# A hybrid decoder step in one program: keys kept transposed for the delta rule, the order of its streams, the memory output stage and the ffn norm

## The chip, the cores and the metric

The kernel runs on one core of a Trainium2 chip. The metric is device time in microseconds for one execution; lower is better. The median of three runs stands for a kernel.

## What is computed

One layer of a decoder for 512 prompt tokens and 32 sample tokens (544 columns), width 1024, in float32. Cut to what matters here:

```python
u = rmsnorm(h); qa, ka, va, qkv_b, z, beta, a, gate_a, gate_b = split(u @ w_in)
A = dilated window attention(qa, ka, va)
q, k, v = silu(causal_dwconv(qkv_b)); q, k = l2norm(q), l2norm(k)
B = gated_delta_chunked(q, k, v, beta, g, s0)      # 8 heads, 128 x 128 state
h += merge(A, B, gates) @ w_out
h += memory_attend(rmsnorm(h)) @ w_mem_o
h += conv_ffn(rmsnorm(h)); y = rmsnorm(h)
```

In the delta rule each head needs, per 128 tokens, a triangular system `M` (built from keys and decay), the values, the keys scaled by decay with tokens on the partitions (`k_dec`), and then a recurrence over four chunks that carries the state `St`.

## The kernel before, in words

All activations lie transposed, 128 features on the partitions and 544 tokens along the row. The weights come as blocks, most of them 128x1024, in the order of `plan()`. Each block is loaded (`wr`), split on ScalarE into a rounded high part `wh` and on VectorE into the rest `wl = wr - wh`, and `dense` (line 567) multiplies it: for each of 8 row groups k, three products (wh·xh, wh·xl, wl·xh) on two halves of 272 columns, so 48 matmuls a block into one of two wide PSUM tiles `pd`. The two split parts have two buffers each (`NHL = 2`), so block n+2 is split once block n has been multiplied.

Everything else is written as generators, the streams: dilated attention, the convolution of a delta head (`conv`, line 1038), the delta rule and the memory attention. After each row group `dense` calls `tick` (line 646). It lets streams take steps, smallest priority number first, while an account of the engines that the builder keeps (`_Account`, line 276) says that the step's inputs are there, that enough SBUF slots of the 53 are free, and that VectorE and ScalarE are no further behind TensorE than `LAG[prio]` us. Where slots run out, `reserve` and `drain` force steps. The order of every engine's instructions is thus fixed when the program is built; the engines then run it in order and wait for semaphores.

The delta rule of a group of four heads: `conv` makes `y`, the convolved q, k or v of a head; it is parked in HBM (`park`, line 501), and for q and k transposed on TensorE and squared for the norm. When q and k of four heads are there, `gdn_group` (line 1088) fetches them (`qk<-park`), builds M and the inner attention, and parks these. It then starts `gdn_solve` (a 32x32 triangular solve on VectorE), two `gdn_preps` and the finals. `gdn_prep` (line 1224) fetches Mt, kT and vT of a head (`ft<-park`), transposes each on TensorE (4 transposes of 128x128 into one PSUM bank), scales the transposed keys on ScalarE into `Kd` and the values into `Vr`, and makes the inverse `U`. `gdn_chain` (line 1321) is the recurrence: `xc` on VectorE from `St`, a product with U, `vn` on ScalarE, products with Kd and At, the new `St` on VectorE. `gdn_sample` does the sample tokens; its wide multiplies `sz` run on GpSimd.

`mem_out` (line 2191) is the output projection of the memory attention, blocks `mo` 0 to 3, two output tiles each: after each of the 8 products, `h += pd` on VectorE (the rows `xr<-xr,pd`, which free the wide tile), and `hstat` makes the split norm input `nh`, `nl` and adds squares to `hacc`. `ffn` (line 2205) starts with block `fg` 0, computes the norm in its midst with `rstd` (sums of squares per token by five products with a column of ones, square root on ScalarE, reciprocal on VectorE) and then `spread`s it over the partitions by five products with the identity; the result `rf` scales every product that follows (`fcb<-pd,rf`).

Of the kernel before, what the change touches and what calls it, by code (L numbers as in the profile page):

```python
# [17 lines left out]
D = 1024  # L18
# [384 lines left out]
class Builder:  # L403
    def __init__(self, nc, tc, I, O, ctx):
        self.nc, self.tc, self.I, self.O = _Engines(nc), tc, I, O
        self.acc = self.nc.acc
        self.clk = self.acc.at
        self.ring = {"b": [], "d": []}
        ec = ctx.enter_context
        self.cp = ec(tc.tile_pool(name="cp", bufs=1))  # L410
        self.wp = ec(tc.tile_pool(name="wp", bufs=1))
        self.sp = ec(tc.tile_pool(name="sp", bufs=1))
        self.tp = ec(tc.tile_pool(name="tp", bufs=1))
        self.pd = ec(tc.tile_pool(name="pd", bufs=2, space=PSUM))
# [4 lines left out]
        self.raw, self.hl = {}, {}  # L419
        self.next_load = self.next_split = 0  # L420
        self.streams, self.stores = [], []
        self.count = {"S": 0, "L": 0}
        self.cur = "b"
        self.nm = 0
        self.flags = {}
        n = 0
        self.src = []
        for b in self.plan:
            if b[0] == "fd":
                self.src.append(I[f"wd{b[1][0]}"][b[1][1]])  # L430
            else:
                self.src.append(I["w"][n]); n += 1
# [94 lines left out]
    def split_to(self, j):  # L527
        while self.next_split <= min(j, len(self.plan) - 1):
            n = self.next_split
            self.load_to(n + NAHEAD)  # L530
# [14 lines left out]
            self.nc.vector.tensor_tensor(lo, r, hi.bitcast(F32), OP.subtract)  # L545
            self.hl[n] = (hi, lo)
            self.hl.pop(n - NHL - 2, None)
            self.next_split += 1

# [11 lines left out]
    def weights(self, b, ahead=True):  # L561
        n = self.idx[b]
        self.split_to(n + (NHL - 1 if ahead else 0))
        return self.hl[n]
# [81 lines left out]
    def tick(self):  # L646
# [3 lines left out]
        self.flush()  # L650
        while c["PE"] - t0 < PE_SHARE:
# [47 lines left out]
    def rstd(self, accs, n):  # L699

        nc = self.nc
        c = (n + 127) // 128
        pb = self.bank((128, c))
        for t in range(c):
            o = min(128 * t, n - 128)
            nc.tensor.matmul(pb[:, t:t + 1], accs[0][:, o:o + 128], self.cst("ones")[:, 0:1], start=True, stop=True)
        return self.rroot(pb)

# [329 lines left out]
    def conv(self, kind, h, cb):  # L1038
# [20 lines left out]
        if kind < 2:  # L1059
            if g not in self.ssT:  # L1060
                self.ssT[g] = self.small(34, tag="w34", bufs=16)
            yield 0, 0
# [4 lines left out]
            for i in range(4):  # L1067
                c = 16 * (1 - kind) + 4 * i + hh
                nc.scalar.activation(self.small(128, tag="junk", bufs=2), pb[:, 128 * i:128 * i + 128], AF.Square, accum_out=self.ssT[g][:, c:c + 1])
        self.flag((kind, h))  # L1070

    def gdn_setup(self):
# [6 lines left out]
        self.ob, self.ssT, self.silz, self.gc = {}, {}, {}, {}  # L1079
# [8 lines left out]
    def gdn_group(self, g):  # L1088
# [89 lines left out]
        self.add(self.gdn_solve(g), 1, (2, 1), (2, 1), "gdn_group")  # L1178
        for e in range(NPREP):
            self.add(self.gdn_preps(g, range(e, 4, NPREP), Mt, At), 1, (3, 0), (6, 0), "gdn_group")  # L1180
# [3 lines left out]
    def gdn_preps(self, g, hs, Mt, At):  # L1184
        pre = None
        for hh in hs:
            if pre is None:
                pre = [self.fetch(d) for d in (Mt[hh], self.sil[1, 4 * g + hh], self.sil[2, 4 * g + hh])]
# [35 lines left out]
    def gdn_prep(self, g, hh, nx, Mts, At, pre):  # L1224
# [7 lines left out]
        Mt, kT, vT = pre[:3]  # L1232
        U = pre[3] if len(pre) > 3 else None
        del pre
        yield from self.on(Mt, kT, vT)
# [7 lines left out]
        yield 1, 0, 3, 0  # L1243
        Kd = self.s((128, 512), name="Kd")
        pb = self.bank()
        for sl in sls:
            nc.tensor.transpose(pb[:, sl], kT[:, sl], ident)
        for i in range(4):
            act(Kd[:, sls[i]], pb[:, sls[i]], AF.Copy, scale=c["kd"][:, cc[i]])
        yield 0, 0, 2, 0  # L1250
        pb = self.bank()
        for sl in sls:
            nc.tensor.transpose(pb[:, sl], vT[:, sl], ident)
        Vr = vT
# [3 lines left out]
        del vT  # L1258
# [55 lines left out]
        if nx is not None:  # L1314
            pre = [self.fetch(d) for d in (Mts[nx], self.sil[1, 4 * g + nx], self.sil[2, 4 * g + nx])] + [self.load_u(g, nx)]
        self.add(self.gdn_chain(g, hh, U, Kd, Vr, At.pop(hh), self.sil[0, h], kT), 1, (2, 0), (2, 0), "gdn_preps")
# [874 lines left out]
    def mem_out(self):  # L2191
        xs = list(zip(self.oh, self.ol))
        self.hstat_begin()
        ps = [self.wide() for _ in range(2)]
# [4 lines left out]
        for m in range(8):  # L2199
            o = ps[m][:, 256:800] if m < 2 else self.dv(self.dense(("mo", m // 2), xs, k0=4 * (m % 2), last=m % 2 == 1))  # L2200
            self.nc.vector.tensor_tensor(self.h[m], self.h[m], o, OP.add)
            self.hstat(m, "g_ffn", self.nc.gpsimd if m < 7 else None)


    def ffn(self):
# [121 lines left out]
    def main(self):  # L2327
# [9 lines left out]
        for n, (kind, k) in enumerate(MIX):  # L2337
# [3 lines left out]
            if kind in "gd" and tag not in seen:  # L2341
# [56 lines left out]
MAIN, PE_SHARE, LAG = 5, 2.5, {0: 4.5, 1: 2.5, 2: 2.5, 3: 1.5}  # L2398
# [52 lines left out]
```

## Time and profile before

| | |
|---|---|
| runs | 1245.27 us median of 3 (1244.31 to 1246.10) |
| profiled execution | 1244.79 us, its span 1243.0 us |
| TensorE busy | 1209.9 us, 97% of the span |
| VectorE, ScalarE, GpSimd busy | 714.5, 527.8, 163.0 us |
| DMA queue of the program | 232.95 MB, 54.4% of 16 engines |
| chain that ended last | TensorE 64%, VectorE 5%, DMA 4%, ScalarE 3%, issue 2% |

A matmul record lasts from its start to a modelled end, and records overlap, so the mean of a record is longer than the distance between two starts. Nearly every instruction has line 339, the recording layer's call; groups are told apart by the tiles they write and read.

### The profile page before, as it was taken

The page shows a single profiled execution, that of the slowest core. Times are in us where ns is not written, and L with a number is a line of the kernel's source. Part 1 is how long each engine was busy: PE and PEld are TensorE (multiplying, and loading weights), DVE is VectorE, ACT ScalarE, POOL GpSimd, SP SyncE. Part 2 cuts the span into 40 slices and gives each one's busy share as a digit, 9 for nine tenths or more (in the row PEclk, how much of TensorE's full clock was granted, in tenths as well). Part 3 has the DMA queues.
Part 4 walks back from the last instruction along what each step waited for, and adds up shares of the span by engine and source line. Part 5 has one row for each costly group of instructions (what it writes and reads, how often), then busy time and mean ns, then how long its engine had stood idle before and what let it go on. Part 6 is the DMA issues. An engine that isn't in the chain of part 4 may idle for free.

```text
span 1243.0 us, 26005 instructions
## 1 busy us (share of the span) xinstructions
PE 1209.9 (97%) x10498; PEld 1164.1 (94%) x10498; DVE 714.5 (57%) x1360; ACT 527.8 (42%) x1128; POOL 163.0 (13%) x352
## 2 busy tenths in 40 slices
PE   7999999999999999999999999999999999999997
PEld 7899998999999988988899998899999999999997
DVE  6635356766688845584675555565552455424564
ACT  5334434555544634665742344453331233313342
POOL 0000100311251220020000000022220022101210
PEclk9999999999999999999999999999999999999998
DMA  6332773446686569746394488364655555555322
GB/s 225 107 118 78 281 264 106 162 145 221 213 262 219 192 196 319 256 146 198 120 326 136 175 311 279 116 218 156 226 182 176 203 187 186 188 193 186 121 84 72
DMA packets 90693, 234.61 MB, mean 189 GB/s; under 512 B 25929, under 2 KB 31542, under 8 KB 89797
## 3 DMA queue, kind: packets, MB, share of 16 engines
q1 hardware_dynamic: 90574, 232.95, 54.4%
q8 instruction: 83, 1.36, 0.4%
q14 instruction: 36, 0.29, 0.1%
HBM read 199.47 MB, written 77.58 MB: 223 GB/s over the span
## 4 chain that ended last, share of the span: by engine, by line
PE 64%; DVE 5%; DMA 4%; ACT 3%; issue 2%; SPq 1%; POOL 0%; POOLq 0%; DVEq 0%; ACTq 0%
PE pd L339 52%; PE b L339 12%; DVE wl L339 1%; DMA z<-park 1%; SPq L339 1%; DMA ft<-park 1%; ACT wh L339 1%; DMA qk<-park 1%; DVE y L339 1%; DMA mkv<-mkT 0%; DVE xr L339 0%; DMA wr<-in_w 0%; DVE st L339 0%; DMA usol<-su 0%; DVE su L339 0%
## 5 line engine op out<-in xcount | busy, mean ns | idle before, releaser
L339 DVE TENSOR_TENSOR wl<-wr,wh 128x1024 fp32r<-128x1024 f32 (+2 forms) x175 | 214.7, 1229 | 215.1 <-ACT wh L339 209.3
L339 ACT ACTIVATE wh<-wr 128x1024 fp32r<-128x1024 f32 (+2 forms) x175 | 177.9, 1020 | 124.3 <-PE pd L339 119.3
L339 PE MATMUL pd<-uh,wh 128*128 128x272 f32 x1008 | 221.1, 301 | 0.9 <-ACT wh L339 0.9
L339 PE MATMUL pd<-uh,wl 128*128 128x272 f32 x1008 | 208.7, 288 | 1.0 <-DVE wl L339 1.0
L339 PE MATMUL pd<-ul,wh 128*128 128x272 f32 x1008 | 208.5, 288 | 0.0
L339 PEld LDWEIGHTS pd<-uh,wh 128*128 128x128 f32 x1008 | 157.2, 189 | 9.5 <-issue 5.0
L339 PE MATMUL pd<-nh,wh 128*128 128x272 f32 (+2 forms) x744 | 159.7, 291 | 0.5 <-DVE xr L339 0.5
L339 PEld LDWEIGHTS pd<-uh,wl 128*128 128x128 f32 x1008 | 158.8, 188 | 1.4 <-DVE wl L339 1.4
L339 PEld LDWEIGHTS pd<-ul,wh 128*128 128x128 f32 x1008 | 159.1, 188 | 0.0
L339 PE MATMUL pd<-nl,wh 128*128 128x272 f32 (+2 forms) x744 | 157.6, 288 | 0.0
L339 PE MATMUL pd<-nh,wl 128*128 128x272 f32 (+2 forms) x744 | 157.5, 288 | 0.0
L339 PEld LDWEIGHTS pd<-nh,wh 128*128 128x128 f32 x744 | 119.0, 188 | 2.9 <-issue 1.9
L339 PEld LDWEIGHTS pd<-nl,wh 128*128 128x128 f32 x744 | 119.0, 188 | 0.2
L339 PEld LDWEIGHTS pd<-nh,wl 128*128 128x128 f32 x744 | 119.1, 188 | 0.0
L339 POOL TENSOR_TENSOR sr<-fy,rf 128x512 f32<-128x512 f32 (+1 forms) x44 | 53.5, 1237 | 69.5 <-ACT fy L339 69.5
L339 DVE SCALAR_TENSOR_TENSOR y<-cb,par,y 128x568 f32<-128x568 f32 x72 | 60.3, 839 | 1.7
L339 PE MATMUL pd<-fl,wh 128*128 128x272 f32 x256 | 53.2, 288 | 0.0
L339 PE MATMUL pd<-fh,wh 128*128 128x272 f32 x256 | 53.2, 288 | 0.0
L339 PE MATMUL pd<-fh,wl 128*128 128x272 f32 x256 | 53.1, 288 | 0.0
L339 DVE SCALAR_TENSOR_TENSOR fy<-fcb,par,fy 128x560 f32<-128x560 f32 x44 | 35.3, 801 | 22.4 <-ACT fy L339 21.7
L339 POOL TENSOR_TENSOR hacc<-hacc,hsq 128x544 f32<-128x544 f32 x6 | 8.2, 1372 | 255.8 <-ACT hsq L339 255.8
L339 PEld LDWEIGHTS pd<-fh,wh 128*128 128x128 f32 x256 | 40.6, 188 | 0.0
(394 smaller groups left out, 2204.1 us busy)
## 6 DMA issues: line engine op xcount, KB each, us to landing
wr<-in_w SPq DMA_DIRECT2D x146, 512.0 KB
out_d<-in_c SPq DMA_DIRECT2D x32, 1022.0 KB
ft<-park SPq DMA_DIRECT2D x40, 256.0 KB
kc<-in_ck SPq DMA_DIRECT2D x18, 512.0 KB
kc<-in_cv SPq DMA_DIRECT2D x18, 512.0 KB
wr<-in_wd SPq DMA_DIRECT2D x16, 512.0 KB
out_d<-in_c SPq DMA_DIRECT2D x8, 1016.0 KB
park<-y SPq DMA_DIRECT2D x24, 256.0 KB
```

The costliest lines, as they stand in the source:

```text
L339: return f(*a, **k)
```

## The change

The keys that `conv` transposes for the norm are now also copied out of PSUM on ScalarE (`tok`, 128x512) and parked in HBM; `gdn_prep` fetches them with Mt, kT and vT and scales them in place, and its four transposes of kT into a bank go away. The priorities move: `gdn_group` 2 to 0, `gdn_solve` 1 to 0, `gdn_chain` 1 to 0, `gdn_sample` 1 to 2; `LAG` goes from 4.5 to 3.5 at priority 0 and from 2.5 to 1.5 at priority 2. In `mem_out` the first two outputs are handled each behind its own product, the split of the next block is started ahead of the add, and its VectorE half (`lows`) is held back until the add is issued. The ffn norm is made by two products of a 128x128 matrix of ones with `hacc` (272 columns each), which give the sums on every partition at once; square root and reciprocal then run on 128x272 twice.

```diff
 def split_to(self, j):
+            self.lows(True)
             self.load_to(n + NAHEAD)
...
             self.nc.scalar.activation(hi, r, AF.Copy)
-            self.nc.vector.tensor_tensor(lo, r, hi.bitcast(F32), OP.subtract)
+            self.late = (lo, r, hi)
+            if not self.defer:
+                self.lows(True)
+    def lows(self, now=False):
+        if self.late and (now or self.acc.ready[_key(self.late[2])][0] <= self.clk["PE"]):
+            lo, r, hi = self.late
+            self.late = None
+            self.nc.vector.tensor_tensor(lo, r, hi.bitcast(F32), OP.subtract)
...
+    def norm(self, acc, r):
+        for e in range(2):
+            pb, sl = self.bank((128, NH)), slice(NH * e, NH * e + NH)
+            self.nc.tensor.matmul(pb, self.cst("ones"), acc[:, sl], start=True, stop=True)
+            self.nc.scalar.activation(r[:, sl], pb, AF.Sqrt, bias=self.eps[:, 0:1], scale=1.0 / D)
+        for e in range(2):
+            sl = slice(NH * e, NH * e + NH)
+            self.nc.vector.reciprocal(r[:, sl], r[:, sl])
...
 def conv(self, kind, h, cb):
-            yield 0, 0
+            yield (1, 0) if kind else (0, 0)
...
+            if kind:
+                tok = self.s((128, 512), name="tok")
+                nc.scalar.activation(tok, pb, AF.Copy)
+                self.tok[kind, h] = self.park(tok)
...
-        self.add(self.gdn_solve(g), 1, (2, 1), (2, 1), "gdn_group")
+        self.add(self.gdn_solve(g), 0, (2, 1), (2, 1), "gdn_group")
...
-            self.add(self.gdn_preps(g, range(e, 4, NPREP), Mt, At), 1, (3, 0), (6, 0), "gdn_group")
+            self.add(self.gdn_preps(g, range(e, 4, NPREP), Mt, At), 1, (4, 0), (6, 0), "gdn_group")
...
 def gdn_prep(self, g, hh, nx, Mts, At, pre):
-        Kd = self.s((128, 512), name="Kd")
-        pb = self.bank()
-        for sl in sls:
-            nc.tensor.transpose(pb[:, sl], kT[:, sl], ident)
         for i in range(4):
-            act(Kd[:, sls[i]], pb[:, sls[i]], AF.Copy, scale=c["kd"][:, cc[i]])
+            act(Kd[:, sls[i]], Kd[:, sls[i]], AF.Copy, scale=c["kd"][:, cc[i]])
...
-        self.add(self.gdn_chain(g, hh, U, Kd, Vr, At.pop(hh), self.sil[0, h], kT), 1, (2, 0), (2, 0), "gdn_preps")
+        self.add(self.gdn_chain(g, hh, U, Kd, Vr, At.pop(hh), self.sil[0, h], kT), 0, (2, 0), (2, 0), "gdn_preps")
...
 def mem_out(self):
+        self.defer = True
+        def done(m, o):
+            if m % 2:
+                self.split_to(self.idx["mo", m // 2] + 2)
+            self.nc.vector.tensor_tensor(self.h[m], self.h[m], o, OP.add)
+            self.lows(True)
+            self.hstat(m, "g_ffn", self.nc.gpsimd if m < 7 else None)
...
-        for m in range(8):
-            o = ps[m][:, 256:800] if m < 2 else self.dv(self.dense(("mo", m // 2), xs, k0=4 * (m % 2), last=m % 2 == 1))
-            self.nc.vector.tensor_tensor(self.h[m], self.h[m], o, OP.add)
-            self.hstat(m, "g_ffn", self.nc.gpsimd if m < 7 else None)
+                if i == 0:
+                    done(m, ps[m][:, 256:800])
+        for m in range(2, 8):
+            done(m, self.dv(self.dense(("mo", m // 2), xs, k0=4 * (m % 2), last=m % 2 == 1)))
+        self.defer = False
...
 def ffn(self):
-                    ps = self.dense(("fg", j), xs, mid=lambda: r.append(self.rstd([self.hacc], N)))
-                    r = self.spread(r[0], N, self.s(name="rf"))
+                    r = self.s(name="rf")
+                    ps = self.dense(("fg", j), xs, mid=lambda: self.norm(self.hacc, r))
...
-                    self.add(self.gdn_group(tag[1]), 2, (2, 0), (8, 0))
-                    self.add(self.gdn_sample(tag[1]), 1, (0, 0), (4, 5))
+                    self.add(self.gdn_group(tag[1]), 0, (2, 0), (8, 0))
+                    self.add(self.gdn_sample(tag[1]), 2, (0, 0), (4, 5))
...
-MAIN, PE_SHARE, LAG = 5, 2.5, {0: 4.5, 1: 2.5, 2: 2.5, 3: 1.5}
+MAIN, PE_SHARE, LAG = 5, 2.5, {0: 3.5, 1: 2.5, 2: 1.5, 3: 1.5}
```

Three places show what moves.

TensorE, the preparation of heads in the second group, before: `ft972` is a head's Mt, `ft970` and `ft973` are kT of two heads, `ft971` is vT; the rest are chain steps of other heads and the block `wh61`.

```order
L339 MATMUL b1021_7217<-ident_107,ft972_6980 128x128 x4
L339 MATMUL b1023_7225<-ident_107,ft970_6976 128x128 x4
L339 MATMUL b1024_7234<-vn1012_7188,Kd866_6469 128x128
L339 MATMUL b1025_7236<-St975_6992,ft949_6869 128x128
L339 MATMUL b1025_7236<-vn1012_7188,ft948_6867 128x128
L339 MATMUL pd1009_7165<-uh70_432,wh61_7047 128x272 x2
L339 MATMUL pd1009_7165<-ul71_433,wh61_7047 128x272 x2
L339 MATMUL pd1009_7165<-uh70_432,wl61_7048 128x272 x2
L339 MATMUL pd1009_7165<-uh73_444,wh61_7047 128x272 x2
L339 MATMUL pd1009_7165<-ul74_445,wh61_7047 128x272 x2
L339 MATMUL pd1009_7165<-uh73_444,wl61_7048 128x272 x2
L339 MATMUL b1027_7255<-ident_107,ft971_6978 128x128 x4
```

TensorE, the same preparation in the change, for another head: `ft1113` is Mt, `ft1116` is vT.

```order
L339 MATMUL b1126_7855<-ident_107,ft1113_7766 128x128 x4
L339 MATMUL pd1129_7875<-uh56_361,wh66_7789 128x272 x2
L339 MATMUL pd1129_7875<-ul57_362,wh66_7789 128x272 x2
L339 MATMUL pd1129_7875<-uh56_361,wl66_7790 128x272 x2
L339 MATMUL pd1129_7875<-uh59_379,wh66_7789 128x272 x2
L339 MATMUL pd1129_7875<-ul60_380,wh66_7789 128x272 x2
L339 MATMUL pd1129_7875<-uh59_379,wl66_7790 128x272 x2
L339 MATMUL pd1129_7875<-uh62_397,wh66_7789 128x272 x2
L339 MATMUL pd1129_7875<-ul63_398,wh66_7789 128x272 x2
L339 MATMUL pd1129_7875<-uh62_397,wl66_7790 128x272 x2
L339 MATMUL b1130_7894<-ident_107,ft1116_7772 128x128 x4
```

The set of four on the keys is gone; over the program TensorE has 32 transposes fewer, and with the ffn norm 9290 matmuls in place of 9330. The program changes between the wide products of the weight blocks and other products 377 times in place of 383.

TensorE, the transposes of the gates' inputs (`ba`, evacuated on VectorE from the block before), before:

```order
L339 MATMUL pd480_3580<-uh78_466,wl34_3446 128x272 x2
L339 MATMUL pd503_3715<-uh56_361,wh35_3576 128x272 x2
L339 MATMUL pd503_3715<-ul57_362,wh35_3576 128x272 x2
L339 MATMUL pd503_3715<-uh56_361,wl35_3577 128x272 x2
L339 MATMUL b507_3727<-ident_107,ba502_3707 128x16 x4
```

In the change they stand at the end of that block, behind 42 of its 48 matmuls instead of 6:

```order
L339 MATMUL pd513_3746<-uh76_456,wh35_3577 128x272 x2
L339 MATMUL pd513_3746<-ul77_457,wh35_3577 128x272 x2
L339 MATMUL pd513_3746<-uh76_456,wl35_3578 128x272 x2
L339 MATMUL b514_3789<-kc492_3655,pz495_3669 32x128 x8
L339 MATMUL b516_3801<-kc494_3667,pz495_3669 32x128 x8
L339 MATMUL b521_3819<-ident_107,ba512_3738 128x16 x4
```

The transposes moved behind 36 more matmuls of the block.

VectorE in `mem_out`, before, from the add of output 1 (`xr1364`) on; `wl101` is the split of the next block, `nl` the low part of the norm's input:

```order
L339 TENSOR_TENSOR xr1364_9340<-xr1364_9340,pd1522_10460 128x544
L339 SCALAR_TENSOR_TENSOR nl1537_10562<-xr1364_9340,par_94,nh1536_10561 128x544
L339 TENSOR_TENSOR wl101_10572<-wr101_10383,wh101_10571 128x1024
L339 TENSOR_TENSOR xr1365_9342<-xr1365_9342,pd1539_10575 128x544
L339 SCALAR_TENSOR_TENSOR nl1541_10602<-xr1365_9342,par_94,nh1540_10601 128x544
```

And in the change:

```order
L339 TENSOR_TENSOR xr1372_9340<-xr1372_9340,pd1530_10460 128x544
L339 TENSOR_TENSOR wl101_10564<-wr101_10383,wh101_10563 128x1024
L339 SCALAR_TENSOR_TENSOR nl1545_10569<-xr1372_9340,par_94,nh1544_10568 128x544
L339 TENSOR_TENSOR xr1373_9342<-xr1373_9342,pd1547_10575 128x544
L339 SCALAR_TENSOR_TENSOR nl1549_10602<-xr1373_9342,par_94,nh1548_10601 128x544
```

`wl101` moved ahead of `nl`; on ScalarE its `wh101` moved ahead of `nh` and the square of the same output.

## Rows read from the trace of the kernel before

**Rows 1.** Page, part 1: engine, busy us (share of the span), instructions.

```profile
PE 1209.9 (97%) x10498; PEld 1164.1 (94%) x10498; DVE 714.5 (57%) x1360; ACT 527.8 (42%) x1128; POOL 163.0 (13%) x352
```

**Rows 2.** Windows: stretch, its us, busy us (instructions) by engine, clock, DMA.

```profile
300.00:400.00 100.00, 97.99 (x974) 94.49 (x976) 77.31 (x159) 53.19 (x142) 32.49 (x72) 1.00 0.70 239
...
500.00:600.00 100.00, 95.38 (x912) 91.03 (x914) 65.36 (x175) 62.44 (x168) 11.24 (x18) 1.00 0.58 192
...
834.00:1190.00 356.00, 356.00 (x2814) 356.00 (x2813) 167.78 (x204) 108.34 (x126) 62.06 (x128) 1.00 0.51 182
```

**Rows 3.** Waits of PE, 60 to 640 us: us in total, times, longest.

```profile
PE b L339 <- DMA qk<-park: 2.2, 1, 2.2
PE b L339 <- DVE y L339: 2.0, 1, 2.0
PE pd L339 <- DVE wl L339: 1.6, 3, 0.6
PE b L339 <- DVE sz L339: 1.3, 2, 0.8
PE b L339 <- DVE xc L339: 1.1, 1, 1.1
PE b L339 <- ACT Kd L339: 1.0, 1, 1.0
PE pd L339 <- ACT wh L339: 0.9, 1, 0.9
PE b L339 <- DVE ba L339: 0.8, 1, 0.8
...
PE pd L339 <- DVE mkT L339: 0.3, 1, 0.3
```

**Rows 4.** Groups by form, PE: count, busy us, mean ns of a record, idle before.

```profile
L339 PE MATMUL b<-ident,y 128*128 128x128 f32 x64 | 9.6, 273 | 2.0 <-DVE y L339 2.0
...
L339 PE MATMUL b<-mkv,cq 128*128 128x256 f32 x32 | 8.4, 385 | 0.4 <-DVE ol L339 0.4
```

**Rows 5.** Groups by form, ACT.

```profile
L339 ACT ACTIVATE Dm<-Dm,qng 128x128 f32<-128x128 f32 x32 | 10.2, 393 | 14.6 <-DVE Dm L339 14.6
...
L339 ACT ACTIVATE pt<-b 128x512 f32<-128x512 f32 x16 | 9.5, 595 | 6.0 <-PE b L339 6.0
L339 ACT ACTIVATE Kd<-b,kd 128x128 f32<-128x128 f32 x32 | 9.2, 372 | 9.6 <-PE b L339 9.5
```

**Rows 6.** Waits of PE, 806 to 850 us.

```profile
PE pd L339 <- DVE xr L339: 1.5, 3, 0.5
```

**Rows 7.** Timeline in the memory output stage: start, us, engine, operation.

```profile
810.49 1.60 DVE L339 TENSOR_TENSOR wl<-wr,wh 128x1024 fp32r<-128x1024 f32 x1 [0.71 <-ACT wh L339]
...
812.01 0.71 DVE L339 TENSOR_TENSOR xr<-xr,pd 128x544 f32<-128x544 f32 x1
...
812.86 0.49 PE L339 MATMUL pd<-oh,wh 128*128 128x272 f32 x2 [0.49 <-DVE xr L339]
```

**Rows 8.** Timeline at the ffn norm.

```profile
831.04 1.17 PE L339 MATMUL b<-ones,hacc 128*128 128x1 f32 x10
832.07 0.50 PE L339 MATMUL pd<-nh,wh 128*128 128x272 f32 x2
...
833.66 1.20 PE L339 MATMUL b<-ident,m 128*128 128x128 f32 x10
834.69 0.49 PE L339 MATMUL pd<-nh,wh 128*128 128x272 f32 x2
...
835.88 0.78 DVE L339 TENSOR_TENSOR fcb<-pd,rf 128x512 f32<-128x512 f32 x2
...
840.84 0.41 PE L339 MATMUL pd<-nh,wh 128*128 128x272 f32 x2
```

**Rows 9.** Groups by form, DVE: the reciprocals.

```profile
L339 DVE RECIPROCAL m<-m 128x1 f32<-128x1 f32 x20 | 3.3, 163 | 19.3 <-ACT sc L339 17.8 <-ACT ssc L339 0.8 <-ACT cp L339 0.7
...
L339 DVE RECIPROCAL m<-m 128x34 f32<-128x34 f32 x3 | 1.1, 360 | 1.0 <-ACT m L339 1.0
```

More of the change, by code (lines that the diff above doesn't have):

```diff
@@ L418, in __init__ @@
         self.idx = {b: n for n, b in enumerate(self.plan)}
-        self.raw, self.hl = {}, {}
+        self.raw, self.hl, self.late, self.defer = {}, {}, None, False
         self.next_load = self.next_split = 0
@@ L563, in weights @@
         self.split_to(n + (NHL - 1 if ahead else 0))
+        if n == self.next_split - 1:
+            self.lows(True)
         return self.hl[n]
@@ L650, in tick @@
         self.flush()
+        self.lows()
         while c["PE"] - t0 < PE_SHARE:
@@ L1066, in conv @@
             del y
-            for i in range(4):
+            if kind:
+                tok = self.s((128, 512), name="tok")
+                nc.scalar.activation(tok, pb, AF.Copy)
+                self.tok[kind, h] = self.park(tok)
+            for i in range(4 if kind < 2 else 0):
                 c = 16 * (1 - kind) + 4 * i + hh
@@ L1078, in gdn_setup @@
         self.sil, self.silS, self.state, self.oraw = {}, {}, {}, {}
-        self.ob, self.ssT, self.silz, self.gc = {}, {}, {}, {}
+        self.ob, self.ssT, self.silz, self.gc, self.tok = {}, {}, {}, {}, {}
         self.msol = [self.dr.tile([64, 32, 32], F32, name=f"msol{g}") for g in range(2)]
@@ L1187, in gdn_preps @@
             if pre is None:
-                pre = [self.fetch(d) for d in (Mt[hh], self.sil[1, 4 * g + hh], self.sil[2, 4 * g + hh])]
+                pre = [self.fetch(d) for d in (Mt[hh], self.sil[1, 4 * g + hh], self.tok[1, 4 * g + hh], self.sil[2, 4 * g + hh])]
                 yield 1, 0, 5, 0
@@ L1231, in gdn_prep @@
         t4 = lambda t: t.rearrange("p (t c) -> p t c", t=4)
-        Mt, kT, vT = pre[:3]
-        U = pre[3] if len(pre) > 3 else None
+        Mt, kT, Kd, Vr = pre[:4]
+        U = pre[4] if len(pre) > 4 else None
         del pre
-        yield from self.on(Mt, kT, vT)
+        yield from self.on(Mt, kT, Kd, Vr)
         pb = self.bank()
@@ L1242, in gdn_prep @@
         v.tensor_copy(t4(C)[64:128, :, 0:96], t4(pb)[64:128, :, 0:96])
-        yield 1, 0, 3, 0
-        Kd = self.s((128, 512), name="Kd")
-        pb = self.bank()
-        for sl in sls:
-            nc.tensor.transpose(pb[:, sl], kT[:, sl], ident)
         for i in range(4):
-            act(Kd[:, sls[i]], pb[:, sls[i]], AF.Copy, scale=c["kd"][:, cc[i]])
+            act(Kd[:, sls[i]], Kd[:, sls[i]], AF.Copy, scale=c["kd"][:, cc[i]])
         yield 0, 0, 2, 0
@@ L1252, in gdn_prep @@
         for sl in sls:
-            nc.tensor.transpose(pb[:, sl], vT[:, sl], ident)
-        Vr = vT
+            nc.tensor.transpose(pb[:, sl], Vr[:, sl], ident)
         for i in range(4):
@@ L1257, in gdn_prep @@
         yield 2, 0, 2, 0
-        del vT
         if U is None:
@@ L1314, in gdn_prep @@
         if nx is not None:
-            pre = [self.fetch(d) for d in (Mts[nx], self.sil[1, 4 * g + nx], self.sil[2, 4 * g + nx])] + [self.load_u(g, nx)]
-        self.add(self.gdn_chain(g, hh, U, Kd, Vr, At.pop(hh), self.sil[0, h], kT), 1, (2, 0), (2, 0), "gdn_preps")
+            pre = [self.fetch(d) for d in (Mts[nx], self.sil[1, 4 * g + nx], self.tok[1, 4 * g + nx], self.sil[2, 4 * g + nx])] + [self.load_u(g, nx)]
+        self.add(self.gdn_chain(g, hh, U, Kd, Vr, At.pop(hh), self.sil[0, h], kT), 0, (2, 0), (2, 0), "gdn_preps")
         del U, Kd, Vr, kT
@@ L2193, in mem_out @@
         self.hstat_begin()
+        self.defer = True
[3 more added lines that the diff above has]
+            self.nc.vector.tensor_tensor(self.h[m], self.h[m], o, OP.add)
+            self.lows(True)
+            self.hstat(m, "g_ffn", self.nc.gpsimd if m < 7 else None)
         ps = [self.wide() for _ in range(2)]
```

## Prediction

> **What bounds the kernel.** The page comes first: TensorE is busy for 1209.9 of 1243.0 us [rows 1]. The windows by stage then say where the other 33 us are: in the ffn TensorE is busy for all of 356 us, with the granted clock at 1.00, the upper of its two levels, while in the stages where the delta rule runs between the weight blocks it idles 2.0 us of 100 (300 to 400 us) and 4.6 us of 100 (500 to 600 us) [rows 2]. VectorE is at 65 to 77% there and DMA at 58 to 70%, so neither is the bound. TensorE runs its instructions in a fixed order; any product taken off it shortens the program by its distance to the next start, and any wait in front of one lengthens it. The waits of TensorE between 60 and 640 us are 14 groups that sum to 13.6 us, from 2.2 us for a fetch to 0.3 us [rows 3]; no cause stands out. What is to be priced is therefore TensorE work that goes, waits that go, and waits that come.
>
> **Keys kept transposed.** 32 transposes leave TensorE (8 heads, 4 each). The nearest operation is the transpose of `y`, of the same form: 64 records, that is 16 sets of four, are busy for 9.6 us, 0.600 us a set, and one record lasts 0.273 us [rows 4]. So starts lie (0.600 - 0.273) / 3 = 0.109 us apart. Most of the sets stand against other products, so I take 32 x 0.109 = 3.5 us; with a tail after each set it would be 8 x 0.600 = 4.8 us. Where only the tail is in question I stay at the lower end, since the products behind the set start before its tail ends. What is added lies elsewhere. ScalarE gets 8 copies of 128x512 from PSUM, 0.595 us each by the same form [rows 5], 4.8 us in all; the 32 scalings stay and read SBUF in place of PSUM, 0.393 us by a scaled SBUF row against 0.372 us [rows 5], 0.7 us. Their cover is that ScalarE is busy for 53 to 62 us of 100 there [rows 2]; if it were gone, 5.5 us. Eight stores and eight fetches of 256 KB are 4.2 MB beside 233 MB, and 16 more issues on SP's queue; they cost nothing unless a fetch is late (a rival below).
>
> The Trainium skill (TensorE: Matmul & The Clock Gate, Part 4: PE-mode transpose) gives about 275 ns for a transpose of 128x128 within a kernel. The 0.273 us of a record agrees with it, but as a duration; by that figure the 32 would be worth 8.8 us, and the row's distance between starts gives 3.5 us.
>
> **Memory output stage.** TensorE waits three times for the add `xr` that frees a wide tile, 1.5 us together [rows 6]. The timeline shows why: the split `wl` (1.60 us) stands on VectorE ahead of the add, which starts at 812.01 as `wl` ends, and the product that needs the tile starts at 812.86 [rows 7]. In the new order the split is begun earlier on ScalarE and stands on VectorE right behind the previous add, so it is over by the time the next product ends; what is late next would be `nl` of the output before, which now waits for one split more on ScalarE, but it is read only some products later. I take 1.5 us; 2.0 us if the restart of TensorE after each wait counts too.
>
> **The ffn norm.** Before, two pieces stand on TensorE's path: 831.04 to 832.07 and 833.66 to 834.69, 2.06 us [rows 8]. The new one is two f32 products of 272 columns. A product of 256 columns (two records each, so 16 of them) takes 8.4 / 16 = 0.525 us [rows 4], so 272 columns 0.56 us and both 1.1 us. Gain 1.0 us (0.9 to 1.2). The reciprocals grow: from 0.163 us for one column and 0.360 us for 34 [rows 9] a column costs 0.0060 us, so 272 columns 1.78 us, an estimate from these two rows, and both 3.6 us in place of about 0.2. The cover: products end near 832.1, the first square root (between the 0.37 and 0.60 us of rows 5) near 832.6, reciprocals end near 836.2, one split at its longest (1.60 us, rows 7) and `fcb` (0.78 us) bring 838.6. Before, `fcb` ended at 836.66 and the block that takes its wide tile started at 840.84 [rows 8], now 839.8. The cover is 1.2 us; without it TensorE would lose what is over.
>
> **The order of the streams.** This has no row, only bounds. Two waits lose their cause: the one for `ba` (0.8 us), whose transposes now stand behind 42 matmuls of the block and not 6, and the one for `Kd` (1.0 us), since no bank waits for that evacuation now [rows 3]. The other 11.8 us are a new draw: each belongs to a place that the new order takes apart. At best all go. Against that, I counted in both orders how many wide matmuls stand between a chain step's producer and the product that reads `vn` or `xc`: at most six at 37 of 56 places before, at 41 now. The chain is packed slightly closer, and the waits that this caused so far (`xc` 1.1 us) would grow a little. Between all gone and none gone I take a quarter gone, 2.7 us, near the lower end for that reason. Together 4.5 us; ends 13.6 us and a loss (below).
>
> **Sum.** 3.5 + 1.5 + 1.0 = 6.0 us that rest on rows, and 4.5 us of waits: 10.5 us off the profiled execution's 1244.8 us, 1234.3 us. The median of the runs lies 0.5 us above that execution, so 1234.8 us. All upper ends (4.8, 2.0, 1.2, 13.6) give 21.6 us and 1223.7 us.
>
> **Rivals.** *Waits only move (0.22).* The new order has as many waits as the old; the 6.0 us remain: 1239.3 us, from 1236 to 1243. For it: before, no cause recurs, so there is nothing that a reordering removes by rule.
>
> *Slower: the splits of the weight blocks fall behind (0.13).* The group, the solve and the chain now come at priority 0, where a step may be taken while VectorE or ScalarE is 3.5 us behind TensorE, and not 2.5. Their steps then stand ahead of `wh` and `wl` of the next block on these two engines, in blocks 39 to 74. TensorE waits 0.6 us at most each time that it meets a late `wl` [rows 3], so ten late blocks use up the 6.0 us, 15 give 1248.3 us, all 36 about 1261 us. For it: VectorE is busiest there, and ScalarE gets 4.8 us more. Against it: three such waits in all before, and convolutions, which were at priority 0 already, may now run ahead less than before.
>
> *Late keys (0.05).* A head's keys now come through HBM. If each of 8 fetches ended as late as the one `qk` fetch that TensorE waited for (2.2 us, rows 3), 17.6 us would be lost: 1256.9 us. Against it: keys are parked some 15 blocks before they are fetched, and in the new order the fetches are issued a block or more before the first use. The Trainium skill (DMA: Bandwidth & Descriptors, Latency and other measured facts) puts most of a DMA's fixed cost, about 2 us, on the answer of the memory, longer under load; two DMAs in a row would be some 4 us, an estimate from that page, and no row here shows the two parts.
>
> *A transpose costs its whole record (0.05).* If each kept TensorE for its 0.273 us, the change would remove 8.7 us with the keys instead of 3.5: 1229.6 us. It is the skill's figure above; against it stands the 0.600 us of a set of four.
>
> *The stages at the end do not give (0.03).* If the first ffn block meets the late reciprocals and the memory output meets `nl`, 2.5 us stay: 1237.3 us.
>
> **Numbers.** The forecast itself has 0.52 (1228 to 1238). A difference under 0.2%, 2.5 us, can't be told from none by a measurement of this kernel; the bounds are 1242.8 and 1247.8 us. Faster: the forecast, 0.19 of the first rival, the last two: 0.79. Same: the rest of the first rival, 0.05 of the second and 0.01 of late keys: 0.09. Slower: 0.08 and 0.04, 0.12. The range that holds 8 in 10 goes from 1228 us to 1244 us: it leaves out the larger part of the second rival, the late keys and the best end.
>
> **What would show it.** Right: no transposes of keys and 9290 matmuls on TensorE; `tok` copies near 0.6 us on ScalarE; no wait of TensorE on `xr` near 810 us; one short piece on `ones` and `hacc` in place of two, reciprocals near 1.8 us, and no wait before the second `fg` block; waits between 60 and 640 us near 9 us, without `ba` and `Kd`. Wrong: many waits on `wl` or `wh` between 290 and 620 us, waits on `ft<-park`, chain waits (`xc`, `vn`, `St`) above 5 us together, or a wait on `fcb`.

## The result, and the profile after

The change made the kernel slower: 1251.84 us median of 20 runs (1243.56 to 1254.63) against 1243.59 us of 20 runs of the kernel before, a ratio of 1.0059 (95% interval 1.0046 to 1.0071). The forecast was 1234.8 us, and its range ended at 1244.

The runs of the change don't scatter evenly. Three of the 20 took 1243.6 to 1244.9 us at a mean granted TensorE clock of 0.994; the other 17 took 1249.3 to 1254.6 us at 0.984 to 0.990. The kernel before, in 80 runs taken beside the experiments, lies between 0.995 and 0.998. So a trace of each kind is needed: "after" below is an execution of the first kind (1243.56 us), and a1_again, the same kernel once more, is one of the second (1254.94 us).

The page of after begins with the line that answers to [rows 1]:

```profile
PE 1211.3 (98%) x10450; PEld 1162.4 (94%) x10450; DVE 720.1 (58%) x1361; ACT 533.4 (43%) x1135; POOL 160.2 (13%) x352
```

Its TensorE is as busy as before, with 48 fewer records. Of what the prediction watched, all but the sum of the waits went as it said, and none of its signs of being wrong came: what it watched had no clock in it. The waits of TensorE from 806 to 850 us, three on `xr` in [rows 6], are none in after; and at the ffn norm the timeline has one short piece on `ones` and `hacc` in place of the two of [rows 8]:

```profile
830.97 1.08 PE L339 MATMUL b<-hacc,ones 128*128 128x272 f32 x4
831.63 0.95 ACT L339 ACTIVATE rf<-b,eps 128x272 f32<-128x272 f32 x2 [1.18 <-PE b L339]
831.69 0.61 PE L339 MATMUL pd<-nh,wh 128*128 128x272 f32 x2
...
832.15 3.56 DVE L339 RECIPROCAL rf<-rf 128x272 f32<-128x272 f32 x2 [1.32 <-ACT rf L339]
...
836.71 0.78 DVE L339 TENSOR_TENSOR fcb<-pd,rf 128x512 f32<-128x512 f32 x2
```

It keeps TensorE from 830.97 to 831.69, 0.72 us in place of 2.06. The copies of the keys on ScalarE (groups by form, ACT) cost what the prediction had:

```profile
L339 ACT ACTIVATE tok<-b 128x512 f32<-128x512 f32 x8 | 4.8, 600 | 10.3 <-PE b L339 10.3
```

What it did not watch stands in the waits of TensorE from 60 to 640 us (answering to [rows 3]) and in the granted clock. The waits, the first six of nine groups:

```profile
PE b L339 <- DVE m L339: 4.7, 1, 4.7
PE b L339 <- DVE xc L339: 1.6, 1, 1.6
PE pd L339 <- DVE wl L339: 1.2, 3, 0.5
PE pd L339 <- ACT wh L339: 1.0, 2, 0.6
PE b L339 <- DMA kc<-in_ck: 1.0, 1, 1.0
PE b L339 <- DVE sz L339: 0.8, 1, 0.8
```

`ba`, `Kd`, `y` and `qk<-park` are gone from the list; one wait of 4.7 us, longer than any before, took their place. The nine groups sum to 12.0 us (12.1 in a1_again) where the prediction had about 9 and the kernel before 13.6. Timelines of after around it, VectorE, GpSimd and TensorE in turn:

```profile
537.08 0.23 DVE L339 TENSOR_TENSOR su<-su,st 128x70 f32<-128x70 f32 x1
537.35 1.79 DVE L339 TENSOR_TENSOR st<-sm,su 128x56 f32<-128x56 f32 x1
539.18 1.82 DVE L339 TENSOR_TENSOR su<-su,st 128x56 f32<-128x56 f32 x1
541.04 1.81 DVE L339 TENSOR_TENSOR st<-sm,su 128x45 f32<-128x45 f32 x1
542.88 1.82 DVE L339 TENSOR_TENSOR su<-su,st 128x45 f32<-128x45 f32 x1
...
545.06 0.28 DVE L339 TENSOR_TENSOR m<-m,b 128x128 f32<-128x128 f32 x1
...
537.17 7.46 POOL L339 TENSOR_TENSOR sz<-sz,eGs 128x1024 f32<-128x1024 f32 x4 [35.41 <-PE b L339]
...
540.25 0.41 PE L339 MATMUL pd<-uh,wl 128*128 128x272 f32 x2
545.40 0.79 PE L339 MATMUL b<-m,m 128*128 128x128 f32 x2 [4.74 <-DVE m L339]
```

`sz`, `m` and `b<-m,m` belong to `gdn_sample` of the second group, `st` and `su` to `gdn_solve`. While the four wide multiplies `sz` run on GpSimd, each step of the solve on VectorE lasts as long as one of them: 1.8 us in place of 0.23. `m` stands in the queue behind them, and TensorE waits. The Trainium skill (GPSIMD Engine Reference, 1. Specifications) says that the two engines share their way to SBUF and that a VectorE operation with two SBUF inputs contends; `st` and `su` are such operations, and the rows agree.

In the trace of the kernel before, the second group's `sz` began at 455 us and its solve at 524 us. In the change, with `gdn_sample` at priority 2 in place of 1 and the solve at 0, the two lie one on the other, at 537 us.

Now the windows of after and then of a1_again, cut where the clock changes (columns as in [rows 2]):

```profile
540.50:545.00 4.50, 0.16 (x2) 0.00 (x0) 4.36 (x5) 0.31 (x2) 4.50 (x4) 1.00 0.09 31
545.10:548.40 3.30, 3.00 (x13) 3.00 (x14) 2.27 (x8) 1.86 (x3) 0.46 (x1) 0.50 0.09 16
548.50:589.30 40.80, 38.27 (x397) 31.85 (x397) 23.71 (x53) 19.27 (x53) 3.96 (x7) 1.00 0.75 246
589.40:592.80 3.40, 3.13 (x14) 2.60 (x13) 1.83 (x5) 3.38 (x11) 1.55 (x3) 0.50 0.44 169
```

```profile
545.30:548.60 3.30, 3.30 (x15) 3.30 (x16) 2.27 (x8) 1.86 (x3) 0.06 (x1) 0.50 0.22 37
548.70:555.50 6.80, 5.96 (x40) 4.31 (x39) 4.32 (x11) 3.25 (x5) 0.00 (x0) 1.00 0.30 53
555.60:572.50 16.90, 16.13 (x113) 11.55 (x116) 8.27 (x18) 0.82 (x4) 0.00 (x0) 0.50 0.78 277
572.60:596.40 23.80, 22.16 (x248) 20.42 (x245) 10.73 (x23) 15.26 (x46) 4.15 (x7) 1.00 0.63 210
596.50:610.10 13.60, 12.54 (x92) 10.95 (x91) 5.05 (x12) 7.49 (x25) 3.20 (x5) 0.50 0.09 35
```

Behind the idle 4.7 us the clock falls to its lower level, 1.2 GHz, in both. The two executions run the same instructions in the same order, to 555 us within 0.3 us of each other. There, in the second, the clock falls again, for 17 us, and once more near 596 us. In the trace of the kernel before it falls only at the end of the program.

Adding up TensorE's distances from start to start over its first 3,500 wide products (to about 660 us) separates the causes. Each instruction is priced at the median distance of its form in the trace of the kernel before, at full clock; what is over is a wait (over 0.25 us), a small excess, or time lost at the low clock (waits inside these stretches included); the first start, near 7 us, is not in the four columns.

| us | instructions | waits | small | at low clock | end of the 3,500th |
|---|---|---|---|---|---|
| before | 584.1 | 25.1 | 41.4 | 0 | 658.2 |
| after | 580.6 | 27.8 | 41.1 | 3.5 | 660.2 |
| a1_again | 580.6 | 23.1 | 39.4 | 20.6 | 671.1 |

The 32 transposes are the 3.5 us in the first column; by the way it is made that is the prediction's own price, 32 times 0.109, and no measurement of it (k1_transposes is one). The other columns carry some noise: e1_ends, whose order is that of the kernel before up to the memory output, has 22.7 us of waits and 40.8 small, 3.0 less than before together. Next to that the waits can't be said to have shrunk, and the low clock costs up to 20.6 us.

### The profile page after: what moved, and what is told of

Its sections match the earlier page's. It is cut to its first block, busy times and chain, and to the rows that moved or that the text cites. A ratio compares the mean times of both kernels' runs of the same rounds, so it can differ in the third digit from the quotient of the medians.

```text
span 1241.8 us, 25949 instructions
## 1 busy us (share of the span) xinstructions
PE 1211.3 (98%) x10450; PEld 1162.4 (94%) x10450; DVE 720.1 (58%) x1361; ACT 533.4 (43%) x1135; POOL 160.2 (13%) x352
## 4 chain that ended last, share of the span: by engine, by line
PE 90%; DVE 4%; ACT 3%; DMA 2%; issue 1%; SPq 0%; POOL 0%; POOLq 0%; DVEq 0%; ACTq 0%
PE pd L339 72%; PE b L339 18%; DVE wl L339 1%; ACT wh L339 1%; DMA z<-park 1%; DMA kc<-in_ck 1%; ACT ft L339 0%; DVE st L339 0%; DVE su L339 0%; ACT L339 0%; DMA kc<-in_cv 0%; ACT m L339 0%; DMA w<-in_w 0%; DVE m L339 0%; DVE sc L339 0%
## 5 line engine op out<-in xcount | busy, mean ns | idle before, releaser
L339 PEld LDWEIGHTS pd<-fh,wl 128*128 128x128 f32 x256 | 40.6, 188 | 0.0
L339 PEld LDWEIGHTS pd<-fl,wh 128*128 128x128 f32 x256 | 40.6, 188 | 0.0
```

The lines of the kernel that those rows point to most:

```text
L339: return f(*a, **k)
```

## The experiments

The edits are shown shortened, `...` marks what is left out. For them, the planner's steps were listed as it takes them. Before, no step of a stream was forced up to the merge (they are taken when they fit). In the change 20 are forced at block 68 (8 of `gdn_chain`, 8 of `gdn_preps`, 4 of `mem_stream`), because the memory keys need `mem_stream` done. That stream began in block 66 and not in 63: room for it is reserved to `gdn_sample` until that ends, in block 66 and not in 58. The theory A of the expectations grew from this.

### The changed kernel again (a1_again)

No edit.

> The changed kernel once more, to have a trace of an execution with the lower mean clock (0.987, as 16 of its 20 timed executions showed; the profiled one had 0.994 and 1243.56 us). Theory A (waits of TensorE that let its clock fall): the trace has about seven stretches at granted clock 0.5 of 3.4 us each in place of two, all between 530 and 650 us and behind waits of TensorE; they account for the 8 us between 1243.6 and 1251.8. Rival B: the clock falls elsewhere, before 530 us or in the ffn, without a wait ahead of it. Rival C: the clock is as in the trace already seen and the 8 us are waits on transfers.

1251.45 us (ratio 1.0048, 1.0027 to 1.0069). Theory A on the place: 34 us at the low clock, all between 545 and 610 us. The theory had seven pieces of 3.4 us, 24 in sum; there are three, of 3.4, 17 and 13.7. By the table the low clock costs 17.1 us more than in after, more than the whole difference of the two traces at the 3,500th product, 10.9. So C falls, and B by its place; but the long fall, at 555.5 us, stands behind a wait of only 0.84 us, and that a wait of its own led to it is not shown.

### The end stages alone (e1_ends)

The kernel before with the change's `split_to`, `lows`, `weights`, `tick`, `mem_out`, `ffn` and `norm`.

> The kernel before with only the new memory output stage and the new ffn norm. From the two traces side by side these two gave 2.1 and 1.3 us; if they do so alone: 1243.6 - 3.4 = 1240.2 us, mean clock 0.997 as in the kernel before. The prediction's own terms (1.5 and 1.0) give 1241.1. If the end stages only seemed to gain because what precedes them ended late: 1243.6.

1238.8 us (0.9964, 0.9951 to 0.9977), mean clock 0.996 to 0.998. By the traces the lead over the kernel before grows by 2.1 us in the memory output and 1.3 in the norm, 3.4 us; the rest of the medians' 5.2 us lies within the interval. These two parts alone beat both kernels.

### The wide multiplies in pieces (e2_pieces)

```diff
-            nc.gpsimd.tensor_tensor(s0[hh], s0[hh], eGs[8 columns], OP.mult)
+            for b in range(8):
+                nc.gpsimd.tensor_tensor(s0[hh][:, b], s0[hh][:, b], eGs[column b], OP.mult)
```

> The changed kernel with each of the eight multiplies sz on GpSimd cut into eight of 128x128; the order on every engine is otherwise the same, row by row. Theory A (the four sz multiplies of the second group, 1.9 us each, hold up VectorE's solve steps st and su, of which four took 1.8 in place of 0.24 us; m stands behind them, and TensorE waited 4.7 us for m): each step of the solve waits for at most one short piece, the wait for m falls under 1.5 us, the fall of the clock behind it goes, and the time falls from 1251.8 to between 1238 and 1246 us, according to how many of the other falls of the clock it caused. Rival B (the clock falls because of the thin work of the chains after 550 us): wait for m gone, but mean clock still 0.987 or 0.988, 1248 us. Rival C (VectorE and GpSimd share a port by bytes, not by instruction): the solve steps are as slow as before in sum, 1251.8 us.

1248.18 us (1.0041, 1.0028 to 1.0054), mean clock 0.987 to 0.989. The wait on `m` is gone, and with it the fall at 545; the solve's steps take 0.31 to 0.33 us beside the pieces. But the clock falls at 551 us, for 17 us:

```profile
547.00:551.00 4.00, 2.86 (x14) 1.09 (x8) 3.06 (x5) 1.55 (x2) 2.92 (x8) 1.00 0.03 5
551.10:568.00 16.90, 14.84 (x110) 10.43 (x114) 7.12 (x17) 0.94 (x4) 0.00 (x0) 0.50 0.83 284
```

So the long wait caused the first fall; with it 3.3 us went by the medians (1251.45 in a1_again, beside it), though the two intervals overlap. Rival B is right about the rest. In this place TensorE is used thinly, by products of few rows or columns with gaps between them: there stand the last products of `gdn_sample`, `b<-vm,m`, which use 32 rows of the array (form 32*128) and of which the fourth waits for `sz` on VectorE, and between the two sets of four some products of the weight block and the small products `U,ft` of the preparation.

### gdn_sample at priority 1 (e3_sample1)

```diff
-                    self.add(self.gdn_sample(tag[1]), 2, (0, 0), (4, 5))
+                    self.add(self.gdn_sample(tag[1]), 1, (0, 0), (4, 5))
```

> The changed kernel with gdn_sample back at priority 1 (one number). The order is drawn anew, and in the second group the solve's steps now stand from block 62 to 66 and the sz multiplies still come within them. Theory A: the time depends on whether m or another operation that TensorE needs stands behind a stretched step: if the long wait is gone, mean clock 0.994 or more and 1238 to 1244 us; if it is there, about 1252. Rival B: mean clock 0.987 and 1250 us whether or not there is a wait over 2 us.

1304.67 us (1.0492, 1.0470 to 1.0514), mean clock 0.966 to 0.971: a miss by 50 us. The new order ends `gdn_sample` later still, in block 68, and 131 steps are forced. TensorE's longest waits, 60 to 660 us:

```profile
PE b L339 <- DVE m L339: 6.1, 1, 6.1
PE pd L339 <- ACT wh L339: 5.3, 3, 2.9
PE b L339 <- DMA qk<-park: 4.3, 1, 4.3
```

A priority is no handle on a place: one number moves the whole order.

### Only mem_stream is forced (f1_memonly)

```diff
         while not all(k in self.flags for k in keys):
+            st = [t for t in self.runnable() if keys == (("mem", 0),) and t["gen"].__name__ == "mem_stream" and self.room(t)]
+            if st:
+                self.step(st[0], "F")
+                continue
             assert self.force(), keys
```

> The changed kernel, with one rule of the planner other: where the keys of the memory attention need the stream mem_stream to be done (block 68), the builder forces the four steps of mem_stream that are missing, and not 20 steps of all streams (8 of gdn_chain, 8 of gdn_preps, 4 of mem_stream; the kernel before forced none there, since mem_stream had ended in block 66). Theory A (the forced steps stand on TensorE without a weight block's product between them, TensorE is thinly used for some 8 us near 590 us, and its clock falls there): the second fall of the clock (3.4 us at 589 us in one trace of the change, 13.7 us at 596 us in the other) is gone, the first (at 545 to 573 us) stays; 1243 to 1247 us, mean clock about 0.990 to 0.992. Rival B (chain steps keep the clock low wherever they stand): the second fall comes a little later, 1250 us and 0.987.

1250.27 us (1.0044, 1.0029 to 1.0059), mean clock 0.986 to 0.994: outside theory A's range, at rival B's time. In its trace the first falls stay (3.4 and 6.8 us). From 569.2 to 596.3 us, where the forced steps had stood, the clock is at 1.00; at 596.4 it falls, for 3.4 us, right behind a wait that the edit itself made. With `mem_stream` late and nothing else forced there, TensorE waits for what that stream makes:

```profile
596.13 0.79 PE L339 MATMUL b<-ones,macc 128*128 128x1 f32 x4 [2.62 <-POOL macc L339]
```

So one cause of a fall may have gone and another come; whether the forced steps of the other streams lower the clock near 590 us is left open by this run.

### The second gdn_sample at priority 0 (f2_sample0), and with pieces (f3_sample0_pieces)

```diff
-                    self.add(self.gdn_sample(tag[1]), 2, (0, 0), (4, 5))
+                    self.add(self.gdn_sample(tag[1]), (2, 0)[tag[1]], (0, 0), (4, 5))
```

> The changed kernel with one number other: gdn_sample of the second group at priority 0 (2 in the change, 1 before). By the builder it ends in block 63 in place of 66, mem_stream begins in block 64 in place of 66, and no step is forced at block 68. Theory A (in the change the late gdn_sample costs twice: its own last products stand thin among the small products of gdn_preps near 550 us, and it holds the large SBUF slots that mem_stream needs, so that 20 steps are forced): both falls of the clock go, mean clock 0.997; the time is that of the kernel before with the new end stages, 1238.8 us, less 3.5 us for the 32 transposes, 1235 us, between 1232 and 1240 by the draw of the waits. Rival B (the thin stretches belong to the kept keys and the chains at priority 0): mean clock 0.990 or less and 1245 us or more.

> The kernel of f2_sample0 with the multiplies sz on GpSimd cut into eight pieces each, the order otherwise the same. Where the four sz multiplies of the second group again stand beside the solve's steps on VectorE, the pieces spare what TensorE waits for that; between nothing and 4 us below f2_sample0. If the pieces are not better there (more instructions on GpSimd, each with its own wait on VectorE): the same within 2 us.

f2: 1243.12 us (0.9992, 0.9982 to 1.0002), mean clock 0.995 to 0.997. f3: 1240.67 us (0.9969, 0.9958 to 0.9980), 0.995 to 0.997. The clock is back, with one fall of 3.4 us left in the trace of f2 and none in that of f3; with the pieces the expected 0 to 4 us came. That the falls come with the late `gdn_sample` of the second group is shown, though the one number moves other streams too. The time missed the expected 1232 to 1240: by the sum above, f3 has 580.6 us of instructions, 26.1 of waits and 43.8 small, e1_ends 584.1, 22.7 and 40.8. The transposes gained 3.5 us, and the order gave 6.4 back at the full clock, 3.4 in waits and 3.0 in small excesses. That is one trace against one, with 3.0 us of noise; by the medians of f3 and e1_ends it would be 3.5 + 1.9 = 5.4. The waits of f3 are on other operations than before:

```profile
PE b L339 <- ACT ft L339: 2.0, 4, 0.6
PE b L339 <- DMA qk<-park: 1.4, 2, 0.7
PE b L339 <- DVE St L339: 1.4, 1, 1.4
PE b L339 <- DVE xc L339: 1.2, 2, 0.9
```

### Kept keys in the old order (e4_keys_oldorder)

The changed kernel with the old priorities of group, solve, chain and sample, and `LAG` as before.

> The changed kernel with the old priorities of gdn_group, gdn_solve, gdn_chain and gdn_sample and the old LAG: the kept keys, the end stages and the convolution's yield as in the change. The builder forces 139 steps (40 at block 68, 88 at block 78, 11 at block 80), since the kept keys hold one SBUF slot more per head and the preparations come late. Theory A (what decides is forced steps, and TensorE's clock falls in them): as e3_sample1 with its 131 forced steps, 1285 to 1320 us, mean clock under 0.975. If the forced steps are harmless and the new priorities cost time by themselves: 1238.8 - 3.5 = 1235 us.

1285.88 us (two runs; 1.0329, 1.0305 to 1.0354), mean clock 0.978. The kept keys hold one slot more per head; without the new priorities the preparations come late and 139 steps are forced. The two parts of the change belong together.

### Useless products (g1_filler)

```diff
             for hh in range(4):
+                for _ in range(3 * g):
+                    nc.tensor.matmul(pbs[hh][:, 0:128], ident, ident, start=True, stop=True)
                 mm(pbs[hh], Kd[32 * hh:32 * hh + 32, :], vm[32 * hh:32 * hh + 32, ...
```

> The kernel of e2_pieces with 24 useless products more on TensorE (128x128, f32; three ahead of each of the eight last products of gdn_sample in the second group, into the bank that the product overwrites); no other row of any engine moves. Theory A (the fall of the clock near 550 us comes from how thinly TensorE is used there, and costs 8.5 us for 17 us at half clock): with the fillers the clock stays up there; their own price is 24 x 0.22 = 5.4 us; 1248.2 + 5.4 - 8.5 = 1245 us, mean clock 0.990 to 0.994 in place of 0.987. A kernel with more work on the engine that sets the time is then faster. Rival B (the clock falls for another reason, or from what follows, the small products of gdn_preps): mean clock 0.987 and 1248.2 + 5.4 = 1253.6 us or more.

`g` is the group, 0 or 1, so the second alone gets them, three ahead of each of its eight thin products.

1248.66 us (1.0048, 1.0034 to 1.0062), mean clock 0.992 to 0.994. The time is between the two theories and level with e2_pieces (0.5 us above it by the medians, within the intervals); the clock decides for A. The windows that answer to those of e2_pieces:

```profile
547.00:551.00 4.00, 4.00 (x18) 2.24 (x18) 1.42 (x3) 0.46 (x1) 1.82 (x5) 1.00 0.10 16
551.10:568.00 16.90, 16.90 (x160) 11.63 (x158) 9.21 (x19) 1.46 (x6) 0.00 (x0) 1.00 0.82 277
```

With every other instruction in its order the clock stays at its upper level here (near 592 us it falls for 6.8 us, as in e2_pieces). So it fell there for how TensorE was used. The Trainium skill (TensorE: Matmul & The Clock Gate, Part 1: The HAM clock gate) says that the clock follows how busy the array has been of late; these runs agree.

What the useless products cost they gave back, but the price is not the expected 5.4 us. The first set of four thin products, e2_pieces and then g1_filler:

```profile
546.65 1.13 PE L339 MATMUL b<-vm,m 32*128 32x512 f32 x6 [0.24 <-DVE vm L339]
548.61 1.12 PE L339 MATMUL b<-vm,m 32*128 32x512 f32 x2 [0.82 <-DVE sz L339]
549.66 0.52 PE L339 MATMUL pd<-uh,wh 128*128 128x272 f32 x2
```

```profile
545.14 0.83 PE L1539 MATMUL b<-ident 128*128 128x128 f32 x6
545.90 1.12 PE L339 MATMUL b<-vm,m 32*128 32x512 f32 x2
...
552.70 0.52 PE L339 MATMUL pd<-uh,wh 128*128 128x272 f32 x2
```

Without fillers three of the four products (two records each) run side by side, in 1.13 us; with fillers between them each runs alone. The set takes 7.56 us in place of 3.01, so the two sets cost some 9 us more (an estimate: 2 x 4.55), about what the clock gave back. Whether the useless products kept the clock up or the thin ones now standing apart, this run does not separate.

### The transposes put back (k1_transposes)

```diff
         for sl in sls:
+            nc.tensor.transpose(pb[:, sl], kT[:, sl], ident)
+        for sl in sls:
             nc.tensor.transpose(pb[:, sl], Vr[:, sl], ident)
```

> The kernel of f3_sample0_pieces with the 32 transposes of the keys put back on TensorE, four ahead of each set of four of the values, into the bank that these overwrite; nothing reads them, and no other row moves. It measures what the 32 transposes cost by themselves: 3.5 us by the distance between their starts (the prediction's term), 1240.7 + 3.5 = 1244.2 us; 4.8 with a tail after each set, 1245.5; 8.7 us if each keeps TensorE for its record (the prediction's rival), 1249.4 us.

1243.42 us, 1.0001 (0.9991 to 1.0012) where f3 had 0.9969: 0.0032 of 1243 us, 4.0 us. The two intervals leave some 2 to 6 us, so the 8.7 us of a whole record each is excluded. Between 3.5 and 4.8 it does not decide: here the four stand right ahead of four more, and a tail after each set can't be seen.

### The end stages with pieces (h1_ends_pieces)

e1_ends with the edit of e2_pieces.

> The kernel of e1_ends (the kernel before with the new end stages) with the multiplies sz on GpSimd cut into eight pieces each, the order otherwise the same. In the kernel before TensorE waited 2.0 us for y near 356 us, while VectorE's operations stood beside the first group's sz multiplies; if the pieces spare that and nothing else, 1238.8 - 2 = 1236.8 us; if VectorE has other work ahead of y, 1238.8.

1245.08 us (1.0014, 1.0004 to 1.0024), a miss: 6 us slower than e1_ends. GpSimd's timelines at the first group, e1_ends and then h1_ends_pieces:

```profile
348.76 8.45 POOL L339 TENSOR_TENSOR sz<-sz,eGs 128x1024 f32<-128x1024 f32 x4 [5.88 <-PE b L339]
357.18 1.78 POOL L339 TENSOR_TENSOR qk<-qk,Gb 128x512 f32<-128x512 f32 x1
```

```profile
347.24 16.03 POOL L1502 TENSOR_TENSOR sz<-sz,eGs 128x128 f32<-128x128 f32 x32 [4.52 <-PE b L339]
363.22 1.28 POOL L339 TENSOR_TENSOR qk<-qk,Gb 128x512 f32<-128x512 f32 x1
```

Pieces let VectorE pass, and take twice as long themselves. What is queued behind them on GpSimd, here the multiply `qk` of `gdn_group`, starts 6 us later. TensorE waited 2.3 us for `m` at 367 us and 1.9 for `qk<-park` at 372, soon behind each of them the clock fell for 3.4 us, and the 2.0 us for `y` that were to be spared are gone; between 350 and 375 us the trace loses 5.5 us against that of e1_ends. (A second wait for `qk<-park`, 2.1 us at 470 us, is also in the trace of the kernel before, and not in that of e1_ends: such a wait comes and goes within one order.)

### A late gdn_sample in the old order (e6_ends_sample2)

e1_ends with `gdn_sample` at priority 2.

> The kernel of e1_ends with gdn_sample at priority 2 and nothing else of the change: no kept keys, the old priorities of group, solve and chain. By the builder no step is forced; the second group's gdn_sample ends in block 60 in place of 58, and its last products stand beside the solve. Theory A (a late gdn_sample is what costs): waits of TensorE on m or sz and, if its last products meet those of gdn_preps, falls of the clock: 1240 to 1250 us, mean clock 0.990 to 0.996. If a late gdn_sample costs only together with the kept keys or the forced steps: 1238.8 us within 2, mean clock 0.997.

1244.98 us (1.0010, 0.9999 to 1.0021), mean clock 0.994 to 0.996, 6 us slower than e1_ends. As theory A: a fall of the clock at 510 us, for 3.4 us, behind two sets of `b<-vm,m`, and waits on `xc` (1.4 us) and `m` (1.1). The largest wait, 2.8 us on `y` near 358 us, stands in the first group and was 2.0 in e1_ends. That one number costs, without kept keys and without a forced step; how much of it is the late `gdn_sample` of the second group is not separated.

## Why the prediction was wrong

- **The bound.** "In the ffn TensorE is busy for all of 356 us, with the granted clock at 1.00": the 1.00 was read off [rows 2] and then held fixed. No term and no rival had a clock that falls. This is the step that failed: where the new order uses TensorE thinly the clock is at 0.50, for 6.8 us in after and 34 us in a1_again, which costs 3.5 and 20.6 us by the table, the latter more than all terms together.
- **The order of the streams.** The prediction followed the streams that came forward (splits behind them, chain steps), and never priced the one that went back, `gdn_sample`. What is queued behind it and what it holds decided: VectorE's `m` behind the solve beside `sz`, its thin products beside the preparation, the room that `mem_stream` needs. The 4.5 us for waits were not there: 25.1 us of waits before, 27.8 and 23.1 in the two traces of the change. (A quarter of the 11.8 us is 2.95, not 2.7; that slip is 0.25 us.) The rival that waits only move was right on this, and would have been near the three runs at clock 0.994 once their two falls are added (1239.3 + 3.5 = 1242.8).
- **How much each is worth.** By the ratios the forecast (1234.8 of 1245.3, 0.9916) missed 1.0059 by 0.0143, 17.8 us. f2, with `gdn_sample` early, is at 0.9992: 0.0067 or 8.3 us came back, the late `gdn_sample` with its falls of the clock and its waits. The other 9.5 us are the order's: waits that did not go, and others that came. This is an estimate, since f2 moves other streams too.
- **Kept keys.** Right: put back, the transposes cost 4.0 us where 3.5 stood. The copies on ScalarE are 4.8 us, and no wait of TensorE in after is on `tok` or on the scaled keys.
- **Memory output and ffn norm.** Right, a little low: 2.1 and 1.3 us where 1.5 and 1.0 stood. The two products on `ones` keep TensorE for 0.72 us, not the 1.1 that records of a nearby form gave. The reciprocals take 1.82 us each by the groups (estimate 1.78), and `fcb` ends at 837.5 us with no wait behind it.
- **The slower rival.** Right in sign, wrong in mechanism: TensorE waited for `wl` three times (1.2 us) and for `wh` twice (1.0), not in ten blocks or more. No fetch of kept keys was late.

Not settled is why the clock falls a second time near 590 us in the change. In after no wide product stands from 584.5 to 593.6 us, where the forced steps are, and the fall comes right behind a wait there:

```profile
589.16 0.61 PE L339 MATMUL b<-xc,U 128*128 128x128 f32 x2 [1.58 <-DVE xc L339]
```

The fall goes when `gdn_sample` comes early (f2); f1 took the forced steps away but made a wait of its own, and a filler there was not tried. Nor is it known why the same instructions let the clock fall at 555.5 us in one execution and not in another.

## What to carry to other kernels

Where TensorE sets the time, its clock is a term of the sum: before products are taken away or spread, look for the stretches where it is used thinly, and ask which stretch a new order will make so. Of a reordering, follow the stream that is put back at least as far as those that come forward: what it holds, and beside what it will land. Take parts that stand at the end of a program by themselves first; here they were the whole gain.

## What was not expected of the hardware

- The same program with the same order differs by 8 us and more from one execution to the next (1243.56 and 1254.94 us in the two traces), because the clock falls in some and not in others behind the same instructions: up to 555 us the traces of after and a1_again agree within 0.3 us, afterwards one runs at 0.50 for 17 us.
- A stretch can be busy by its records and still keep the low clock: 16.13 of 16.90 us in a1_again. Records are longer at the low level (`b<-vm,m` 1.22 us in place of 0.69), so the busy share does not warn; the clock column does.
- VectorE and GpSimd took turns by instruction: a step of 0.23 us became 1.8 us beside multiplies of 1.9 us, and 0.32 us beside pieces (e2). The pieces take longer, 16.03 us in place of 8.45 (h1).
- Thin products that use different rows of the array run side by side: three `b<-vm,m` take 1.13 us together, and 1.12 us each where useless products stand between them.
